# Layer 1's projections cut into half tiles and placed between attention units, with their subtractions on VectorE

## The chip, the cores and the metric

One core of one Trainium2 chip. Times are microseconds (us) of device time for one launch of the whole program. Engines: PE (TensorE matmul; PEld is its weight load), DVE (VectorE), ACT (ScalarE), POOL (GpSimd), SP (SyncE, which issues the loads). A time of day such as 892.30 counts from the first instruction of the profiled execution.

## The reference

A transformer of two layers on 256 latent and 256 context tokens of width 1024, in float32. Layer 0 mixes tokens with a window attention and a latent attention, layer 1 with a differential attention; after each comes a hierarchical mixture of 32 experts (top 2 per token). The change is in the mixer of layer 1:

```
h   = modulate(norm(x))                  512 tokens x 1024
q   = rope(h_lat @ Wq)                   256 latent tokens, 8 heads x (2 x 64)
k   = rope(h @ Wk) for the latent tokens, plain for the context tokens
v   = h @ Wv
for head, for each of 2 blocks of 128 queries:
    a1, a2 = softmax(q1 k1 / 8), softmax(q2 k2 / 8)     128 x 512 each
    o      = (a1 - lambda * a2) @ v                     128 x 128
out = rmsnorm(o) * (1 - lambda_init) @ Wout
```

## The kernel before, in words

**Precision.** Every product with weights is made of three matmuls on two halves of each float32 operand, a rounded one ("hi") and the remainder ("lo"). `mm3` (L395) issues them at L401 to L403, `split` (L385) makes the halves: ACT casts to hi (L391), and DVE or POOL subtracts (L394).

**Buffers and loads.** SBUF holds a pool of 24 buffers of 1 MB. `budget(n)` keeps n of them for data, the rest take weights; SP issues loads in one fixed order whenever a buffer comes free. PSUM has three rotating banks under the name psB, so that the fourth tile put there waits until the first has been read.

**Layer 1's mixer.** The MoE of layer 0 ends, h is made, and then two parts follow each other. First the projections: 12 weight tiles of 1 MB in the order `DWO` (0 to 3 make q, 4 to 7 k, 8 to 11 v). The first is multiplied while h is made (into psA); for each of the others `q_tile`, `k_tile` or `v_tile` (L1687 to L1718) makes two halves, each 24 matmuls of 512 columns (k), 24 of 256 (q) or 48 of 256 (v) into one bank of psB. A finished half of k or q is turned by `rope_lat` (L567): one multiply (L571), four on 32 partitions (L574) and an addition (L575), all on DVE; ACT copies the context half of k (L1683), and `split` with POOL as its engine makes the halves of the result. A finished half of v is copied by ACT (L1716). The next tile's weights are split by `W1.get`, `W1.step` and `W1.make`: two casts of 128x1024 on ACT and two subtractions of 128x1024 on DVE per tile.

Then the attention: `run_units` (L797) goes over 16 units (8 heads, 2 query blocks) as a software pipeline of three stages. One turn does for three neighbouring units: scores (`d_scores`, six matmuls of 512 columns, L1743) and row maxima (DVE, L1750, L1751) of unit i+2; the product with v (`d_pv`, L1787) of unit i-1, with its square on ACT (L1790) and its scaling on DVE (L1791); the combination of the two softmax halves (`d_scale`, DVE, L1765, L1766, L1768) of unit i+1; the transposition (`d_transpose`, L1775, copied by ACT, L1777) of unit i; and the exponentials (ACT, L1758) of unit i+2. `fill()` puts four matmuls of a later table (L323) between them. A hook `early1(i)` sets budgets, splits two tiles of the output projection's weights on POOL (`Wo.step(GP, GP)` at i = 7, 9, 11, 13: L393 and L394 on POOL), and begins the norm of the result (L1799 to L1811) in the last turns.

Then the output projection (`out_block`), the router (`ffn_in`) and the MoE of layer 1, whose expert weights (`in_ew_dram`) stream in until the end.

```
    for j in DWO[1:]:
        (q_tile, k_tile, v_tile)[j // 4](j % 4)
    ...
    run_units([(h, qt) for h in range(8) for qt in range(2)], d_scores, d_max, d_exp, d_scale, d_transpose, d_pv,
              lambda i: i in (1, 2, 3, 14, 15), early1, 3)
```

Of the kernel before, what the change touches and what calls it, by code (L numbers as in the profile page):

```python
# [115 lines left out]
def model_kernel(ctx: ExitStack, tc: tile.TileContext, xin, small, cst, ada0, adaw, win, wuq, wukv, wout0, dwin,  # L116
# [24 lines left out]
    def free(n):  # L141
        st_["data"] -= n
# [41 lines left out]
    def U(shape=(512,), dt=F32):  # L184
        return up.tile([P] + list(shape), dt, tag="u", name="u")
# [7 lines left out]
    def psB():  # L193
        return psb.tile([P, 512], F32, tag="B", name="psB")
# [268 lines left out]
    def xc(c):  # L463
        return xmap[c]
# [99 lines left out]
    DVE.tensor_copy(UB, csv("U"))  # L564


    def rope_lat(ps, dst, p0, cosn, sinn):  # L567

        t = U((SEQ,))
        r = U((SEQ,))  # L570
        DVE.tensor_tensor(t[p0:P], ps[p0:P, 0:SEQ], csv(cosn)[p0:P], ALU.mult)  # L571
        for q in range(p0 // 32, 4):
            a, b = slice(32 * q, 32 * q + 32), slice(32 * (q ^ 1), 32 * (q ^ 1) + 32)
            DVE.tensor_tensor(r[b], ps[a, 0:SEQ], csv(sinn)[a], ALU.mult)  # L574
        DVE.tensor_tensor(dst[p0:P, 0:SEQ], t[p0:P], r[p0:P], ALU.add)  # L575
# [1088 lines left out]
    for c in range(KC):  # L1664
# [13 lines left out]
    DVE.tensor_scalar(nlam, lamt[:, 2:3], -LAMBDA_INIT, None, op0=ALU.add)  # L1678
    k1 = [[S((4, NTOK), F32R) for _ in range(2)] for _ in range(2)]

    def k_out(j, ps):
        dst = U()
        ACT.copy(dst[:, SEQ:], ps[:, SEQ:])  # L1683
        rope_lat(ps, dst, 0, "cosA", "sinA")
        split(*(x[j // 4].v[:, j % 4, :] for x in k1), dst, GP)

    def k_tile(j2):  # L1687
        ws = W1.get()
        for j in range(2):
            ps = psB()  # L1690
            s = slice(j * P, (j + 1) * P)
            mm3(ps, KC, lambda k: (ws[0][:, k, s], ws[1][:, k, s]), h13)
            k_out(2 * j2 + j, ps)
        free(2)

    def q_tile(j2):
        ws = W1.get()
        for j in range(2):
            ps = psB()
            s = slice(j * P, (j + 1) * P)  # L1700
            mm3(ps[:, 0:SEQ], KC, lambda k: (ws[0][:, k, s], ws[1][:, k, s]),
                lambda k: tuple(x[:, 0:SEQ] for x in h13(k)))
            dst = U((SEQ,))
            rope_lat(ps, dst, 0, "cosA", "sinA")
            split(*(x.v[:, 2 * j2 + j, :] for x in q1), dst, GP)
        free(2)

    def v_tile(j):
        ws = W1.get()
        for t2 in range(2):  # L1710
            ps = psB()
            for t in range(2):
                ts_ = slice((2 * t2 + t) * P, (2 * t2 + t + 1) * P)
                mm3(ps[:, t * 256:(t + 1) * 256], KC, lambda k: tuple(x[:, ts_] for x in h13(k)),
                    lambda k: (ws[0][:, k, :], ws[1][:, k, :]))
            ACT.copy(v1[j // 2].v[:, 2 * t2:2 * t2 + 2, (j % 2) * 256:(j % 2 + 1) * 256],  # L1716
                     ps.rearrange("p (t n) -> p t n", t=2))
        free(2)  # L1718
# [8 lines left out]
    free(2)  # L1727
    q1 = [S((KC, SEQ), F32R) for _ in range(2)]
    v1 = [S((4, 512)), S((4, 512))]
    budget(18)  # L1730
    for j in DWO[1:]:
        (q_tile, k_tile, v_tile)[j // 4](j % 4)
    free(4)
    oD = S((16, P))
    budget(11)

    def d_scores(u):
        h, qt = u
# [8 lines left out]
    def d_max(u, ps):  # L1747
        st = T((8,))
        for i in range(2):
            DVE.tensor_reduce(out=st[:, i:i + 1], in_=ps[i], axis=AX.X, op=ALU.max)  # L1750
        DVE.tensor_scalar(st[:, 2:4], st[:, 0:2], -0.125, None, op0=ALU.mult)  # L1751
        return ps, st

    def d_exp(u, ps, st):
        res = []
        for i in range(2):
            pt = U()
            ACT.activation(pt, ps[i], AF.Exp, bias=st[:, 2 + i:3 + i], scale=0.125, accum_out=st[:, 4 + i:5 + i])  # L1758
            res.append(pt)
        return res, st  # L1760
# [21 lines left out]
    def d_pv(u, PTs):  # L1782
        h, qt = u
        PT, rec = PTs
        ps = psB()
        for b in range(4):
            PE.matmul(ps[:, 0:P], PT[:, b * P:(b + 1) * P], v1[h // 4].v[:, b, (h % 4) * P:(h % 4 + 1) * P],  # L1787
                      start=(b == 0), stop=(b == 3))
        sq = U((P,))
        ACT.activation(sq, ps[:, 0:P], AF.Square, scale=rec, accum_out=ssD[:, 0, 2 * h + qt:2 * h + qt + 1])  # L1790
        DVE.tensor_scalar(oD.v[:, 2 * h + qt, :], ps[:, 0:P], rec, None, op0=ALU.mult)  # L1791

# [18 lines left out]
        DVE.scalar_tensor_tensor(out=lo, in0=ps, scalar=sl1, in1=hi.bitcast(F32), op0=ALU.mult, op1=ALU.subtract)  # L1811

    def early1(i):
        if i in {2: 13, 10: 14}:
            budget({2: 13, 10: 14}[i])
        if i == 9:
            free(3)
            budget({2: 13, 10: 14}[10])
        if i in (7, 9, 11, 13):
            Wo.step(GP, GP)  # L1820
        if i == 14:

# [211 lines left out]
```

## Time and profile before

| | us |
|---|---|
| median of three runs | 1468.54 |
| lowest and highest run | 1467.93, 1470.87 |
| the profiled execution's own time | 1465.41 |
| its span, first to last instruction | 1463.6 |
| busy: PE, DVE, ACT, POOL | 1304.4, 582.8, 372.8, 139.6 |
| projections of layer 1, from the second tile's first matmul to the first scores | 789.78 to 892.30 |
| attention, from the first scores to the first matmul of the output projection | 892.30 to 958.33 |

1.8 us of the profiled execution lie around its span, and it is 3.1 us below the median of the runs. The chain of waits names, step by step, what the end of the program hung on; the timeline gives every instruction with its start, its duration and, in brackets, how long its engine had been idle; the table of windows gives each engine's busy time in a stretch, the clock that PE was granted (1.00 is full) and the share of time that the load engines were busy. A matmul's duration in the timeline overlaps the next one's, so PE's pace is read from starts.

### The profile page before, as it was taken

What the parts mean: (1) busy time and instruction counts of PE and PEld (TensorE: products, weight loads), DVE (VectorE), ACT (ScalarE), POOL (GpSimd) and SP (SyncE); (2) the same over time, 40 slices, a digit from 0 to 9 for tenths busy, and PEclk for the clock granted to TensorE, in tenths of its full rate; (3) what the DMA queues carried; (4) which work ended last, traced back from release to release, by engine and by line L of the source; (5) the groups of instructions that cost most, each with busy time, mean ns of one, the idle gap of its engine ahead of it and who ended that gap; (6) DMA issues with size and microseconds to landing.
All of it is one profiled execution on the core that took longest, in us unless ns stands there. A gap on an engine that the chain in (4) does not pass through costs nothing.

```text
span 1463.6 us, 21798 instructions
## 1 busy us (share of the span) xinstructions
PE 1304.4 (89%) x8439; PEld 719.5 (49%) x8439; DVE 582.8 (40%) x1423; ACT 372.8 (25%) x800; POOL 139.6 (10%) x129
## 2 busy tenths in 40 slices
PE   7998999989999989989879999797998786878966
PEld 4775669935435343525226896593442321323313
DVE  6577883454232313222237757945311120111102
ACT  4445653331111110101024334743110100101002
POOL 1122341210000000000013201211000000000000
PEclk9999999999999999999999999999999998998989
DMA  9834443489999999999998138357999999999995
GB/s 381 324 115 145 178 163 151 180 341 371 412 420 420 421 421 421 421 420 421 409 413 342 66 115 320 149 221 296 422 421 421 420 421 421 422 421 422 421 410 225
DMA packets 70253, 486.77 MB, mean 333 GB/s; under 512 B 7681, under 2 KB 7937, under 8 KB 13697
## 3 DMA queue, kind: packets, MB, share of 16 engines
q1 hardware_dynamic: 70144, 485.32, 81.6%
q8 instruction: 69, 1.13, 0.3%
q14 instruction: 40, 0.32, 0.1%
HBM read 484.24 MB, written 1.05 MB: 332 GB/s over the span
## 4 chain that ended last, share of the span: by engine, by line
DMA 26%; PE 15%; DVE 6%; ACT 2%; issue 1%; SPq 0%; DVEq 0%; ACTq 0%
DMA s<-in_ew_dram 25%; PE psA L1358 3%; PE psA L1390 2%; PE psB L402 2%; PE psB L403 2%; PE psB L401 2%; DMA s<-in_adaw_dram 1%; DVE t L1750 1%; DVE u L1768 1%; PE psA L401 1%; PE psA L402 1%; PE psA L403 1%; DVE s L394 1%; DVE u L574 0%; DVE t L1751 0%
## 5 line engine op out<-in xcount | busy, mean ns | idle before, releaser
L1358 PE MATMUL psA<-s 128*32 128x512 f32 (+2 forms) x2336 | 420.0, 624 | 78.1 <-DMA s<-in_ew_dram 72.6
L1358 PEld LDWEIGHTS psA<-s 128*32 128x32 f32 (+2 forms) x2336 | 114.8, 122 | 359.7 <-issue 205.2
L1400 DVE SCALAR_TENSOR_TENSOR s<-psB,modT,s 128x256 f32<-128x256 f32 x296 | 120.4, 476 | 214.3 <-PE psB L1407 214.2
L1390 PE MATMUL psA<-s,u 128*32 128x512 f32 (+1 forms) x1168 | 186.7, 607 | 12.4 <-DMA s<-in_ew_dram 10.9
L1395 DVE SCALAR_TENSOR_TENSOR u<-psA,t,u 128x512 fp32r<-128x512 f32 x48 | 36.0, 750 | 233.1 <-ACT u L1394 233.1
L1390 PEld LDWEIGHTS psA<-s,u 128*32 128x32 f32 (+1 forms) x1168 | 53.7, 120 | 123.6 <-issue 96.7
L1407 PE MATMUL psB<-u 128*128 128x512 f32 (+1 forms) x384 | 95.7, 369 | 13.2 <-DVE s L1400 4.8
L1532 DVE TENSOR_TENSOR u<-u,psA 128x512 f32<-128x512 f32 x24 | 16.5, 687 | 224.1 <-PE psA L1358 224.1
L401 PE MATMUL psB<-s 128*128 128x256 f32 (+1 forms) x304 | 98.8, 325 | 0.2 <-DVE s L890 0.2
L1384 ACT COPY u<-psB 128x512 f32<-128x512 f32 x24 | 14.1, 586 | 332.1 <-PE psB L1382 332.1
L402 PE MATMUL psB<-s 128*128 128x256 f32 (+1 forms) x304 | 98.1, 323 | 0.4 <-DVE s L394 0.4
L403 PE MATMUL psB<-s 128*128 128x256 f32 (+1 forms) x304 | 98.0, 322 | 0.0
L1407 PEld LDWEIGHTS psB<-u 128*128 128x128 f32 x384 | 58.8, 188 | 72.4 <-issue 36.0
L1394 ACT ACTIVATE u<-psA,t 128x512 fp32r<-128x512 f32 x48 | 33.0, 687 | 177.4 <-PE psA L1390 171.8
L1529 ACT ACTIVATE u<-psA 128x512 f32<-128x512 f32 x24 | 14.4, 598 | 219.4 <-PE psA L1358 219.4
L1341 PE MATMUL psB<-s 128*128 128x256 f32 x544 | 68.0, 285 | 0.6 <-ACT u L1384 0.6
L394 DVE TENSOR_TENSOR s<-s 128x1024 fp32r<-128x1024 f32 (+3 forms) x56 | 51.6, 966 | 39.2 <-ACT s L391 39.1
L1341 PEld LDWEIGHTS psB<-s 128*128 128x128 f32 x544 | 65.9, 191 | 2.6 <-issue 1.6
L401 PEld LDWEIGHTS psB<-s 128*128 128x128 f32 x304 | 57.9, 190 | 8.3 <-issue 1.7
L402 PEld LDWEIGHTS psB<-s 128*128 128x128 f32 x304 | 57.9, 190 | 4.8 <-DVE s L394 0.7
L403 PEld LDWEIGHTS psB<-s 128*128 128x128 f32 x304 | 57.9, 190 | 4.5
L401 PE MATMUL psA<-s 128*128 128x256 f32 (+1 forms) x200 | 58.7, 294 | 0.0
(354 smaller groups left out, 1706.5 us busy)
## 6 DMA issues: line engine op xcount, KB each, us to landing
s<-in_ew_dram SPq DMA_DIRECT2D x376, 1024.0 KB, 19.8
s<-in_adaw_dram SPq DMA_DIRECT2D x40, 1024.0 KB, 6.6
s<-in_dwin_dram SPq DMA_DIRECT2D x12, 1024.0 KB, 10.5
s<-in_ada_dram SPq DMA_DIRECT2D x8, 1024.0 KB, 17.5
s<-in_wout_dram SPq DMA_DIRECT2D x8, 1024.0 KB, 8.6
s<-in_ew_dram SPq DMA_DIRECT2D x16, 512.0 KB, 14.6
s<-in_win_dram SPq DMA_DIRECT2D x4, 1024.0 KB, 20.9
s<-in_xin_dram SPq DMA_DIRECT2D x4, 512.0 KB, 5.0
```

Of the source, the lines that this page charges most:

```text
L394: eng.tensor_tensor(lo, src, hi.bitcast(F32), ALU.subtract)
L401: PE.matmul(ps, lh, rh, start=(k == 0), stop=False)
L402: PE.matmul(ps, lh, rl, start=False, stop=False)
L403: PE.matmul(ps, ll, rh, start=False, stop=(k == n - 1))
L1341: PE.matmul(ps[:, i * n:(i + 1) * n], src(t, cs_(c0 + i)), oh[:, t, 0:n], start=(t == 0 and a == 0), stop=(t == T_ - 1 and a == 1))
L1358: PE.matmul(ps[sl, :], xg(hf * 4 + k, sl), wt(m, hf)[:, k, :], start=(hf == 0 and k == 0), stop=(hf == 1 and k == 3))
L1390: PE.matmul(ps[sl, :], ht[:, k, sl], wt(2, hf)[:, k, :], start=(k == 0), stop=(k == 3))
L1394: ACT.activation(yh, ps, AF.Copy, scale=gsl)
L1395: DVE.scalar_tensor_tensor(out=yl, in0=ps, scalar=gsl, in1=yh.bitcast(F32), op0=ALU.mult, op1=ALU.subtract)
L1400: DVE.scalar_tensor_tensor(out=xc(c)[:, HALF[s]], in0=ps[:, HALF[s]], scalar=modT[:, l, 5, c, s:s + 1], in1=xc(c)[:, HALF[s]], op0=ALU.mul ...
L1407: PE.matmul(ps[:, 0:nt], ysp[a][:, cs_(q)], oht[:, 0:nt], start=(a == 0), stop=(a == 1))
L1532: TT(hm, sl, pm[1], ALU.mult)
```

## The change

- The projections of tiles 2 to 12 become 22 half tiles, called pieces. A piece is the matmuls of one half into one bank of psB, followed by `W1.step()`, which splits half of the weights of the tile after it (cast on ACT, subtraction on DVE). Its rope or copy (`evacs`) is issued at the start of the next turn, the halves of its result (`splits`) at that turn's end.
- Of tiles 2 to 12 only six halves still precede the unit loop: two halves of q come first, then the scores of units 0 and 1 between two halves of k, two more halves of q, and the other 16 halves stand in turns 0 to 12 of the unit loop, by the table `PIECES`. `DWO` is reordered so that each head's q, k and v come shortly before their use.
- The subtractions that make the lo halves of q and k move from POOL to DVE (8 of 128x512, 8 of 128x256).
- `rope_lat`'s temporaries, q's result and the squares of `d_pv` go to a free half of an old tensor (`room()`), not to the pool of small tiles.
- `Wo.step(GP, GP)` moves from turns 7, 9, 11, 13 to the ends of turns 12 to 15; the fills from three before the loop and turns 1, 2, 3, 14, 15 to turns 2, 6, 11, 13, 14, 15; the budgets to 19 before the attention, 16 at turn 9 and 14 at turn 14 (before 18, 11, 13, 14).

The diff, cut to its core:

```diff
+PIECES = {0: 2, 1: 1, 2: 1, 3: 1, 4: 2, 5: 2, 6: 1, 7: 1, 8: 2, 9: 1, 10: 1, 12: 1}
-DWO = (4, 5, 6, 8, 0, 7, 9, 1, 10, 2, 11, 3)
+DWO = (4, 0, 5, 1, 8, 9, 6, 2, 10, 7, 3, 11)
...
-        split(*(x[j // 4].v[:, j % 4, :] for x in k1), dst, GP)
+        split(*(x[j // 4].v[:, j % 4, :] for x in k1), dst)
...
+    def k_piece(j2, j, ws):
+        ps = psB()
+        s = slice(j * P, (j + 1) * P)
+        mm3(ps, KC, lambda k: (ws[0][:, k, s], ws[1][:, k, s]), h13)
+        dst = []
+
+        def evac():
+            dst.append(U())
+            k_rope(dst[0], ps)
+        return evac, lambda: k_split(2 * j2 + j, dst[0])
...
+    def piece(n=1):
+        for _ in range(n):
+            j, i = pieces.pop(0)
+            if i == 0:
+                cur.append(W1.get(False))
+            made.append((q_piece, k_piece, v_piece)[j // 4](j % 4, i, cur[0]))
+            W1.step()
+            if i:
+                cur.pop()
+                free(2)
...
-    budget(18)
-    for j in DWO[1:]:
-        (q_tile, k_tile, v_tile)[j // 4](j % 4)
-    free(4)
     oD = S((16, P))
-    budget(11)
...
+    piece(2)
+    evacs()
+    splits()
+    for i in range(2):
+        piece()
+        mx1[i] = d_max(units[i], d_scores(units[i]))
+        ex1[i] = d_exp(units[i], *mx1.pop(i))
+    evacs()
+    pts1[0] = d_scale(units[0], ex1.pop(0))
+    splits()
+    piece(2)
+    for i in range(n_u + 1):
+        evacs()
+        if i + 2 < n_u:
+            mx1[i + 2] = d_max(units[i + 2], d_scores(units[i + 2]))
+        early1(i)
+        if 0 < i:
+            d_pv(units[i - 1], PT1.pop(i - 1))
+        if i in (2, 6, 11, 13, 14, 15):
+            fill()
+        if i + 1 < n_u:
+            pts1[i + 1] = d_scale(units[i + 1], ex1.pop(i + 1))
+        if i < n_u:
+            PT1[i] = d_transpose(units[i], pts1.pop(i))
+        if i + 2 < n_u:
+            ex1[i + 2] = d_exp(units[i + 2], *mx1.pop(i + 2))
+        splits()
+        if i in (12, 13, 14, 15):
+            Wo.step(GP, GP)
+        piece(PIECES.get(i, 0))
```

Lines of the changed kernel are two (in the helpers) to some 30 higher than before: the subtraction of `split` is L396 (before L394), the rope L572, L575, L576 (before L571, L574, L575), the scores L1775, the maxima L1782 and L1783, `d_scale` L1797 to L1800, the transposition L1807, `d_pv`'s scaling L1823.

DVE's order from the weights of the second tile on, before (128x8x128 is half a weight tile, that is 128x1024; the first two ropes read psA and belong to the first tile):

```order
L394 TENSOR_TENSOR s<-s 128x8x128 x2
L571 TENSOR_TENSOR u<-psA,u 128x256
L574 TENSOR_TENSOR u<-psA,u 32x256 x4
L575 TENSOR_TENSOR u<-u 128x256
L571 TENSOR_TENSOR u<-psA,u 128x256
L574 TENSOR_TENSOR u<-psA,u 32x256 x4
L575 TENSOR_TENSOR u<-u 128x256
L394 TENSOR_TENSOR s<-s 128x8x128 x2
L571 TENSOR_TENSOR u<-psB,u 128x256
```

and in the changed kernel:

```order
L396 TENSOR_TENSOR s<-s 128x8x128 x2
L572 TENSOR_TENSOR s<-psA,u 128x256
L575 TENSOR_TENSOR s<-psA,u 32x256 x4
L576 TENSOR_TENSOR u<-s 128x256
L396 TENSOR_TENSOR s<-u,s 128x512
L572 TENSOR_TENSOR s<-psA,u 128x256
L575 TENSOR_TENSOR s<-psA,u 32x256 x4
L576 TENSOR_TENSOR u<-s 128x256
L396 TENSOR_TENSOR s<-u,s 128x512
L396 TENSOR_TENSOR s<-s 128x8x128 x2
L572 TENSOR_TENSOR s<-psB,u 128x256
```

The two new rows are k's subtractions (128x512), each after its rope; the third tile's weights come behind both.

DVE a little later in the changed kernel, where the maxima of units 0 and 1, the rest of the third and the fourth tile's weights, and the ropes of two halves of k follow each other (s<-s 128x256 x2 are q's subtractions); before, no unit's work stands among the ropes:

```order
L396 TENSOR_TENSOR s<-s 128x256 x2
L396 TENSOR_TENSOR s<-s 128x8x128
L1782 TENSOR_REDUCE t<-psA 128x1 x2
L1783 TENSOR_SCALAR t<-t 128x2
L396 TENSOR_TENSOR s<-s 128x8x128
L1782 TENSOR_REDUCE t<-psA 128x1 x2
L1783 TENSOR_SCALAR t<-t 128x2
L572 TENSOR_TENSOR s<-psB,u 128x256
L575 TENSOR_TENSOR s<-psB,u 32x256 x4
L576 TENSOR_TENSOR u<-s 128x256
```

The rope of the first of these halves of k now stands behind two units' maxima and two weight subtractions.

PE's order in the middle of the attention before, two whole turns:

```order
L1775 MATMUL psB<-identR,u 128x128 x4
L1743 MATMUL psA<-s 128x512 x6
L1787 MATMUL psB<-s,u 128x128 x4
L1775 MATMUL psB<-identR,u 128x128 x4
L1743 MATMUL psA<-s 128x512 x6
L1787 MATMUL psB<-s,u 128x128 x4
```

and in the changed kernel where the second half of tile 1 (q) ends, turn 0 runs, and the first half of tile 8 (v) begins:

```order
L405 MATMUL psB<-s 128x256
L1775 MATMUL psA<-s 128x512 x6
L1807 MATMUL psB<-identR,u 128x128 x4
L403 MATMUL psB<-s 128x256
L404 MATMUL psB<-s 128x256
L405 MATMUL psB<-s 128x256
```

Scores of unit 2 and the transposition of unit 0 stand between 24 matmuls of a half of q and 48 of a half of v.

## Rows read from the trace of the kernel before

**Rows 1.** windows: length, busy PE, PEld, DVE, ACT, POOL, then PEclk, DMA, GB/s

```profile
850.00:875.00 25.00, 25.00 (x211) 25.00 (x210) 13.78 (x22) 8.26 (x11) 1.48 (x2) 1.00 0.29 88
900.00:925.00 25.00, 19.66 (x130) 12.54 (x130) 23.88 (x41) 13.01 (x37) 14.43 (x8) 0.89 0.80 322
925.00:950.00 25.00, 22.69 (x155) 15.78 (x153) 22.31 (x59) 21.93 (x64) 0.00 (x0) 0.98 0.31 117
1100.00:1436.00 336.00, 268.13 (x1446) 90.67 (x1444) 48.65 (x122) 28.17 (x50) 1.90 (x1) 0.93 1.01 420
```

**Rows 2.** timeline of PE (start, duration): k and q halves, scores, last product with v

```profile
789.78 0.39 PE L401 MATMUL psB<-s 128*128 128x512 f32 x1
795.22 0.39 PE L401 MATMUL psB<-s 128*128 128x512 f32 x1
...
877.33 0.28 PE L403 MATMUL psB<-s 128*128 128x256 f32 x1
880.21 0.28 PE L403 MATMUL psB<-s 128*128 128x256 f32 x1
...
892.30 1.65 PE L1743 MATMUL psA<-s 64*128 64x512 f32 x12
893.88 2.78 PE L323 MATMUL psC<-s,scS 128*32 128x512 f32 x24
...
954.98 1.06 PE L1787 MATMUL psB<-s,u 128*128 128x128 f32 x8
```

**Rows 3.** timeline of PE in one turn of the attention

```profile
907.01 0.66 PE L1775 MATMUL psB<-identR,u 128*128 128x128 f32 x4
907.60 0.96 PE L1743 MATMUL psA<-s 64*128 64x512 f32 x6
908.49 1.16 PE L1787 MATMUL psB<-s,u 128*128 128x128 f32 x8
909.58 1.06 PE L323 MATMUL psC<-s,scS 128*32 128x512 f32 x8
```

**Rows 4.** chain of waits in order of time, one turn apart

```profile
930.64 0.75 DVE u L1768
933.41 0.75 DVE u L1768
```

**Rows 5.** timeline of DVE, ACT and POOL where the projections begin

```profile
788.69 2.36 DVE L394 TENSOR_TENSOR s<-s 128x1024 fp32r<-128x1024 f32 x2
790.97 0.42 DVE L571 TENSOR_TENSOR u<-psA,u 128x256 f32<-128x256 f32 x1
793.16 0.42 DVE L575 TENSOR_TENSOR u<-u 128x256 f32<-128x256 f32 x1
793.66 0.62 ACT L391 CAST s<-u 128x512 fp32r<-128x512 f32 x1 [3.81 <-issue]
797.99 1.30 POOL L394 TENSOR_TENSOR s<-u,s 128x512 fp32r<-128x512 f32 x1 [2.34 <-ACT s L391]
798.90 1.47 DVE L394 TENSOR_TENSOR s<-s 128x1024 fp32r<-128x1024 f32 x1 [1.70 <-ACT s L391]
```

**Rows 6.** groups by line and form, 790 to 990: count, busy, mean ns

```profile
L394 POOL TENSOR_TENSOR s<-u,s 128x512 fp32r<-128x512 f32 x8 | 10.4, 1294 | 33.1 <-ACT s L391 33.1
L575 DVE TENSOR_TENSOR u<-u 128x256 f32<-128x256 f32 x16 | 6.8, 425 | 0.6
L1803 DVE TENSOR_TENSOR s<-s,ssD 128x512 f32<-128x512 f32 x4 | 2.7, 685 | 0.0
```

**Rows 7.** timeline while POOL splits the output projection's weights

```profile
910.82 2.37 POOL L394 TENSOR_TENSOR s<-s 128x1024 fp32r<-128x1024 f32 x1 [2.56 <-PE psC L323]
911.02 2.71 DVE L1768 SCALAR_TENSOR_TENSOR u<-u,t 128x512 f32<-128x512 f32 x1
921.19 1.12 PE L1775 MATMUL psB<-identR,u 128*128 128x128 f32 x4 [4.77 <-DVE u L1768]
```

**Rows 8.** windows, just after PE's idle 4.77

```profile
920.00:926.00 6.00, 4.78 (x19) 3.42 (x20) 5.89 (x9) 2.00 (x6) 4.39 (x3) 0.50 0.10 18
```

More of the change, by code (lines that the diff above doesn't have):

```diff
@@ L50 @@
 ADL = 3
-DWO = (4, 5, 6, 8, 0, 7, 9, 1, 10, 2, 11, 3)
-ADO = {0: (0, 1), 1: (2, 3, 4), 2: (5,), 3: (6,), 4: (7,)}
+PIECES = {0: 2, 1: 1, 2: 1, 3: 1, 4: 2, 5: 2, 6: 1, 7: 1, 8: 2, 9: 1, 10: 1, 12: 1}
+DWO = (4, 0, 5, 1, 8, 9, 6, 2, 10, 7, 3, 11)
+ADO = {0: (0, 1), 1: (2, 3, 4), 6: (5,), 9: (6,), 11: (7,)}
 NFIX = (4, 4)
@@ L564, in model_kernel, with rope_lat @@
     DVE.tensor_copy(UB, csv("U"))
-    def rope_lat(ps, dst, p0, cosn, sinn):
-        t = U((SEQ,))
-        r = U((SEQ,))
+    def rope_lat(ps, dst, p0, cosn, sinn, tr=None):
+        t, r = tr or (U((SEQ,)), U((SEQ,)))
         DVE.tensor_tensor(t[p0:P], ps[p0:P, 0:SEQ], csv(cosn)[p0:P], ALU.mult)
@@ L1672, in model_kernel @@
     h_lo(1, KC - 1, xb, *h13(KC - 1), True)
+    budget(19)
     fill(2)
@@ L1679, in model_kernel, with room, k_rope @@
     k1 = [[S((4, NTOK), F32R) for _ in range(2)] for _ in range(2)]
+    rooms_ = [0]
+    def room():
+        rooms_[0] += 1
+        return xc(rooms_[0] % KC)[:, SEQ:]
+    def k_rope(dst, ps):
+        ACT.copy(dst[:, SEQ:], ps[:, SEQ:])
+        rope_lat(ps, dst, 0, "cosA", "sinA", (room(), room()))
     def k_out(j, ps):
         dst = U()
-        ACT.copy(dst[:, SEQ:], ps[:, SEQ:])
-        rope_lat(ps, dst, 0, "cosA", "sinA")
-        split(*(x[j // 4].v[:, j % 4, :] for x in k1), dst, GP)
@@ L1687, in k_tile @@
[L1687 to L1718, printed above, removed]
+        k_rope(dst, ps)
@@ new lines, in k_out, with k_split, q_piece @@
+        k_split(j, dst)
+    def k_split(j, dst):
+        split(*(x[j // 4].v[:, j % 4, :] for x in k1), dst)
[8 more added lines that the diff above has]
+        return evac, lambda: k_split(2 * j2 + j, dst[0])
+    def q_piece(j2, j, ws):
+        ps = psB()
+        s = slice(j * P, (j + 1) * P)
+        mm3(ps[:, 0:SEQ], KC, lambda k: (ws[0][:, k, s], ws[1][:, k, s]),
+            lambda k: tuple(x[:, 0:SEQ] for x in h13(k)))
+        dst = room()
+        tr = (room(), room())
+        return (lambda: rope_lat(ps, dst, 0, "cosA", "sinA", tr),
+                lambda: split(*(x.v[:, 2 * j2 + j, :] for x in q1), dst))
@@ new lines, in v_piece @@
+    def v_piece(j, t2, ws):
+        ps = psB()
+        for t in range(2):
+            ts_ = slice((2 * t2 + t) * P, (2 * t2 + t + 1) * P)
+            mm3(ps[:, t * 256:(t + 1) * 256], KC, lambda k: tuple(x[:, ts_] for x in h13(k)),
+                lambda k: (ws[0][:, k, :], ws[1][:, k, :]))
+        return (lambda: ACT.copy(v1[j // 2].v[:, 2 * t2:2 * t2 + 2, (j % 2) * 256:(j % 2 + 1) * 256],
+                                 ps.rearrange("p (t n) -> p t n", t=2)), lambda: None)
+    pieces = [(j, n) for j in DWO[1:] for n in range(2)]
@@ L1720, in model_kernel, with evacs, splits @@
+    cur, made = [], []
+    def piece(n=1):
[8 more added lines that the diff above has]
+                free(2)
+    def evacs():
+        for e, _ in made:
+            e()
+    def splits():
+        for n in range(len(made)):
+            made.pop(0)[1]()
     wl = [W1.get(False)]
@@ L1788, in d_pv @@
                       start=(b == 0), stop=(b == 3))
-        sq = U((P,))
+        sq = room()[:, 0:P]
         ACT.activation(sq, ps[:, 0:P], AF.Square, scale=rec, accum_out=ssD[:, 0, 2 * h + qt:2 * h + qt + 1])
@@ L1813, in early1 @@
     def early1(i):
-        if i in {2: 13, 10: 14}:
-            budget({2: 13, 10: 14}[i])
         if i == 9:
             free(3)
-            budget({2: 13, 10: 14}[10])
-        if i in (7, 9, 11, 13):
-            Wo.step(GP, GP)
+            budget(16)
+        if i == 14:
+            free(4)
+            budget(14)
         if i == 14:
@@ L1831, in early1 @@
             d_turn(1)
-    run_units([(h, qt) for h in range(8) for qt in range(2)], d_scores, d_max, d_exp, d_scale, d_transpose, d_pv,
-              lambda i: i in (1, 2, 3, 14, 15), early1, 3)
+    units = [(h, qt) for h in range(8) for qt in range(2)]
+    n_u, ex1, mx1, pts1, PT1 = len(units), {}, {}, {}, {}
+    piece(2)
[28 more added lines that the diff above has]
+        piece(PIECES.get(i, 0))
     d_rstd(12, 16)
```

## The prediction

> **What bounds the kernel now.** I read the table of windows first. From 1100 to 1436 the load engines are busy all the time (1.01, 420 GB/s) and PE is not [rows 1]: layer 1's MoE waits for its expert weights, so nothing saved there counts. It can start only when the mixer before it is done, and the pool of buffers is full by then; so a microsecond that the mixer gains or loses moves the end by about one. The mixer has two regimes. In the projections PE is the bound: 25.00 of 25 busy, DVE 13.78 [rows 1]. In the attention DVE is: 22.31 and 23.88 of 25, PE 22.69 and 19.66 [rows 1]. The change mixes the two.
>
> Next PE's timeline, for its pace (from starts, since durations overlap). A half of k takes 795.22 - 789.78 = 5.44 us, a half of q 880.21 - 877.33 = 2.88, and a half of v, twice q's matmuls, 5.76; a unit's scores half of 893.88 - 892.30, 0.79 [rows 2]. A transposition is 0.59, a product with v 1.09, a fill about 1.0 [rows 3]. So a unit is 2.47 us of PE. The chain shows the pitch of an undisturbed turn, 933.41 - 930.64 = 2.77, carried by DVE [rows 4].
>
> Then DVE's timeline where the projections begin: half a tile's weight subtraction 1.18 (2.36 for two), a rope 2.61 (790.97 to 793.58), of which 2.18 until it has read its bank [rows 5].
>
> **The change, part by part.** PE's own work from 789.78 to the last product with v: six halves of k 32.6, eight of q 23.0, eight of v 46.1, 16 units 39.5, six fills 6.0; together 147.2. Nothing of this is removed: only waits can go. Without any, the last product would end at 937.0; before, it ends at 956.0 [rows 2].
>
> To see the waits I laid the new order end to end by hand: three queues (PE, DVE, ACT), each block in its place in the changed order, starting when its engine is free and 0.12 after its inputs (ACT's cast starts 0.08 after the rope that it reads [rows 5]). DVE's blocks besides those above: a unit's two maxima with their scaling 1.40 and its combination 1.11, which with 0.26 for the product's scaling make the 2.77.
>
> The new subtractions on DVE are not in the trace. The nearest rows are additions on DVE, 0.685 for 128x512 and 0.425 for 128x256 [rows 6]: eight of each are at most 8.9 us, and at least nothing, where DVE would be idle anyway. I lay them at 0.64 and 0.40, a little under, because consecutive instructions of DVE overlap by some 0.03: 8.3 us.
>
> The start. At 788.69 DVE has before it: the second tile's weights 2.36; two halves of k of the first tile, each now rope 2.61, a wait for ACT's cast 0.8, subtraction 0.64, 4.0 in all; then the third tile's first half of weights 1.18. That is 800.3 (788.69 + 2.36 + 8.1 + 1.18). PE, which has two halves of q meanwhile, is done with them at 795.5 and wants those weights: a wait of 5.0. Before, PE had a whole tile of k (10.9) at this place to cover it.
>
> Next come the other half of these weights, two ropes of q, q's subtractions, the fourth tile's weights, two maxima and the rope of the first half of k: scores 0 wait 1.4, and the second half of the next tile of q, which takes the bank of that half of k, three places behind it, waits 3.2. Then two ropes, a combination, subtractions, weights: the first half of v waits for the bank of q's half until 830.7, 5.2; the transposition before it 0.5. Altogether PE has done 25.4 us of work by then, and waited 15.3. DVE's queue, not PE's, sets this stretch: 37 us of blocks in 42.
>
> The middle: in turns 3 to 9 the same happens on a smaller scale wherever halves of k and q follow each other: 0.6, 1.3, 3.6 (the weights of a tile of v stand behind two ropes), 0.6, 1.3, 2.1 (scores 12 wait for the subtraction of q made a turn before), 1.2: 10.7. From turn 13 on no projections are left, and each turn waits 1.0, as before, DVE being the bound: 3.1. Smaller ones 1.0. Waits in all 30.1, so the last product ends at 967.3.
>
> The same lay-out of the kernel before ends at 946.7, where the trace has 956.0. Up to unit 3 it is within 1 us; what it lacks is the 7 us that POOL costs, and 2.3 of the norm in the last turns. Like for like the change costs 967.3 - 946.7 = **20.6**.
>
> POOL's seven: while it subtracts 128x1024 (2.37), DVE's combination takes 2.71 instead of 0.75, and PE then stands idle 4.77 [rows 4, 7]. The changed order sends these four steps later: two fall beside halves of v, on which PE has work for 5.76, two into the last turns. Below, 0 (all hidden); above, 7 as before; I take 3, since half of them meet turns without cover. So 7 are returned and 3 paid.
>
> SP's loads: as many as before, the mixer's twelve in another order; those behind them are released later, because the projections hold their buffers longer. The expert weights that fill the pool are at most some 23 MB, about 55 us at 420 GB/s [rows 1]; the attention's last turns, the output projection and the router, in which they can come, are about as long. I price this at 0, up to 3 if the pool is not full.
>
> The ropes' temporaries in the free half of an old tensor: same instructions, 0. The fills are moved, not removed: 0.
>
> Sum: 20.6 - 7 + 3 = 16.6. Against the profiled execution's 1465.41 this is 1482.0. That execution lies 3.1 below the median, so the median I forecast is **1485**.
>
> **A rule against the change.** POOL's subtraction beside DVE's makes DVE's 1.47 instead of 1.18 [rows 5], and POOL is nearly idle in the projections, 1.48 of 25 [rows 1]. With q's and k's subtractions left on POOL (1.29 [rows 6], and for half the width some 0.7) my lay-out ends at 966.4, 0.9 earlier. The Trainium skill, Perfetto Trace Analysis, section "Optimizing Scalar/DVE Operations", says that if VectorE is saturated it may pay to give work away, even to GPSIMD, but warns that those two share a read port. By its first half the sum would be 15.7 and not 16.6, by its second the 0.29 is the price of that; either way the choice of engine decides less than the order.
>
> **The rivals.**
>
> *Interleaving works* (faster). DVE is busy 13.8 of 25 in one regime and about 23.1 in the other [rows 1]: of 102.5 us of projections and 66 of attention 56 and 61, with the new subtractions 126 us of DVE against 147.2 of PE. If DVE's backlog never reaches PE, the 30.1 of waits go, apart from the last turns' 3.1: 1485 - 27 = 1458. The sign turns where waits fall under 13.5 (30.1 - 16.6). For it: the totals; the weights are split a tile ahead. Against: up to the first half of v DVE has one and a half times PE's work, and three banks let PE run ahead by three halves only. The Trainium skill, Perfetto Trace Analysis, "Optimization Strategy", says that kernels with several regimes may gain by interleaving them; by that rule this case would be the outcome.
>
> *Half of it* (no change). The lay-out overstates the waits by two, at the start and in the middle alike, because a bank or a weight half comes free earlier than I count: 15 are left, about 1470.
>
> *The clock falls* (slower still). After 4.77 idle PE was granted 0.50, the level of 1.2 GHz, for 6 us [rows 7, 8], and a transposition took 1.12 instead of 0.66 [rows 3, 7]. Two waits here are as long. If each is followed by 6 us at half pace, 3 us each, and POOL costs its whole 7, it is 1485 + 6 + 4 = 1495.
>
> *Not what it says*: the weights are a whole tile ahead only in the middle; at the start the third tile's wait for DVE is part of the forecast. I give it no chance of its own.
>
> **How the numbers follow.** Forecast 0.58, its own range 1477 to 1493 (hand-over 0.05 or 0.2: -2.5, +3; POOL 0 to 7; loads 0 to 3). The clock 0.12, interleaving works 0.18, half of it 0.12. The range that leaves out 2 in 10 is 1464 to 1495: it loses most of the interleaving case above and a little of the clock's. A measurement can tell 0.2% here, 2.9 us; 1465.6 to 1471.5 is "same". Half of the "half of it" case lies there; its rest is split between the sides. Faster 0.21, same 0.06, slower 0.73.
>
> **What would show it.** Right: in PE's timeline, idle of about 5 us before the first half of k of the third tile, released by the weight subtraction on DVE, and of 3 to 5 us before the second tile of q and the first half of v, released by ropes; DVE busy 90% from 790 to 830; output projection at about 970 to 973; MoE loads back to back until about 1453. Wrong: PE's busy share over 95% from 790 to 950, with the output projection before 955; or the first projections waiting for something other than DVE, a load of weights above all; or the end moving by another amount than the start of the output projection.

## The result, and the profile after

| | before | after |
|---|---|---|
| median of five runs, us | 1468.54 | 1481.76 |
| lowest, highest | 1463.05, 1470.87 | 1478.95, 1484.62 |
| the profiled execution's own time | 1465.41 | 1481.76 |

The ratio is 1.008, with an interval of 1.0059 to 1.0102: **slower by 9 to 15 us**. The forecast was 1485, in a range of 1464 to 1495.

The page's first lines after:

```profile
span 1480.0 us, 21765 instructions
PE 1309.3 (88%) x8439; PEld 723.4 (49%) x8439; DVE 589.1 (40%) x1439; ACT 372.6 (25%) x800; POOL 122.9 (8%) x113
```

One window over the whole stage, from the first matmul of the second tile to the first of the output projection, shows the difference best. Before (length, then busy PE, PEld, DVE, ACT, POOL, granted clock, load share, GB/s):

```profile
789.78:958.33 168.55, 155.93 (x1089) 131.58 (x1088) 124.20 (x244) 76.80 (x172) 30.68 (x24) 0.98 0.46 174
```

and after, where the stage begins 3.4 later (MoE 0 before it ends at a slightly different time in each execution, 786.4 to 793.3 in the profiles of this study, so stages are compared by their own length):

```profile
793.22:974.86 181.64, 161.01 (x1089) 134.21 (x1088) 131.47 (x258) 76.70 (x172) 13.99 (x8) 0.96 0.37 134
```

The stage grew from 168.55 to 181.64, by 13.1. PE's idle time in it grew from 12.6 to 20.6, by 8.0, and its busy time by 5.1, with the same 1089 matmul instructions (seven fills in each): its granted clock is 0.96 instead of 0.98. From the output projection's first matmul to the last instruction it is 505.3 before and 505.1 after: what the stage loses, the end loses, as the chain shows, which still ends with expert weights back to back:

```profile
1412.84 20.43 DMA s<-in_ew_dram
1433.29 19.87 DMA s<-in_ew_dram
1453.20 3.63 PE psA L1391 x26
```

PE's idle time in its timeline of the changed kernel (start, duration, instruction, and in brackets the idle time before it and who ended it); these answer to [rows 2, 3]:

```profile
802.92 0.79 PE L403 MATMUL psB<-s 128*128 128x512 f32 x1 [3.74 <-ACT s L393]
824.74 0.36 PE L403 MATMUL psB<-s 128*128 128x256 f32 x1 [2.54 <-DVE s L575]
831.46 0.38 PE L403 MATMUL psB<-s 128*128 128x256 f32 x1 [0.67 <-ACT u L1809]
832.42 0.39 PE L404 MATMUL psB<-s 128*128 128x256 f32 x1 [0.58 <-DVE s L396]
...
890.05 0.39 PE L403 MATMUL psB<-s 128*128 128x256 f32 x1 [3.01 <-ACT s L393]
891.31 0.58 PE L404 MATMUL psB<-s 128*128 128x256 f32 x1 [0.87 <-DVE s L396]
...
934.67 1.25 PE L1775 MATMUL psA<-s 64*128 64x512 f32 x6 [1.15 <-ACT s L393]
...
966.88 0.63 PE L1840 MATMUL psB<-identR,s 128*128 128x128 f32 x4 [1.94 <-DVE s L1835]
```

Each is a place of the lay-out: the third tile's first half of k behind its weights (forecast 5.0, measured 3.7), the second half of q behind a rope (3.2, 2.5), the first half of v (5.2, and here 0.7 + 0.6), a half of v behind its weights (3.6, 3.0 + 0.9), scores 12 behind the halves of q (2.1, 1.2, released by ACT's cast). What the lay-out did not have is the clock. In the windows after three of these waits (columns as above) it is at 0.50, the level of 1.2 GHz, or on its way:

```profile
802.00:805.00 3.00, 2.04 (x4) 1.23 (x5) 2.75 (x3) 1.82 (x2) 0.00 (x0) 0.52 0.44 186
805.00:808.00 3.00, 3.00 (x8) 2.32 (x8) 2.85 (x8) 0.05 (x1) 0.00 (x0) 0.50 0.00 0
...
826.00:829.00 3.00, 3.00 (x16) 2.88 (x14) 2.80 (x8) 1.13 (x2) 0.00 (x0) 0.50 0.01 3
...
890.00:893.00 3.00, 2.07 (x9) 1.87 (x10) 2.95 (x4) 0.95 (x2) 0.00 (x0) 0.64 0.79 236
```

With the rows beside these (0.84 from 808 to 811, 0.79 from 893 to 896) busy time at the lower level cost about 6 us, an estimate from these windows (3.0 of 805 to 808 at half pace are 1.5, and so on). A part of the first half of v's forecast wait went there: PE was slower and came later. The half also came free sooner than the lay-out had it, 38.2 after the stage's first matmul (831.46 - 793.22) and not 40.9 (830.7 - 789.78).

Why PE waits at 802.92 is seen in the timeline of ACT and DVE ahead of it; the rows of before are [rows 5]:

```profile
797.17 0.62 ACT L393 CAST s<-u 128x512 fp32r<-128x512 f32 x1 [3.87 <-issue]
797.82 0.69 DVE L396 TENSOR_TENSOR s<-u,s 128x512 fp32r<-128x512 f32 x1 [0.73 <-ACT s L393]
800.79 0.43 DVE L576 TENSOR_TENSOR u<-s 128x256 f32<-128x256 f32 x1
801.30 0.62 ACT L393 CAST s<-u 128x512 fp32r<-128x512 f32 x1 [3.25 <-DVE u L576]
801.83 1.99 ACT L393 CAST s<-s 128x1024 fp32r<-128x1024 f32 x2
801.95 0.69 DVE L396 TENSOR_TENSOR s<-u,s 128x512 fp32r<-128x512 f32 x1 [0.74 <-ACT s L393]
802.90 1.23 DVE L396 TENSOR_TENSOR s<-s 128x1024 fp32r<-128x1024 f32 x1 [0.25 <-ACT s L393]
```

Both queues hold the third tile's weights behind the second rope of k: ACT casts them at 801.83, after the cast of that rope's result, and DVE subtracts them at 802.90, after its subtraction. What releases PE at 802.92 is the first of ACT's casts, not DVE's subtraction. The new subtractions took 0.69 and 0.42 each (0.64 and 0.40 were assumed).

POOL's four subtractions are still there. One lay beside turn 11 of the changed kernel:

```profile
947.28 2.38 POOL L396 TENSOR_TENSOR s<-s 128x1024 fp32r<-128x1024 f32 x1 [9.29 <-PE psC L325]
947.35 2.85 DVE L1800 SCALAR_TENSOR_TENSOR u<-u,t 128x512 f32<-128x512 f32 x1
950.25 0.66 PE L1807 MATMUL psB<-identR,u 128*128 128x128 f32 x4 [0.57 <-DVE u L1800]
...
951.43 2.17 DVE L1783 TENSOR_SCALAR t<-t 128x2 f32<-128x2 f32 x1
```

DVE's combination took 2.85 instead of 0.75, as it took 2.71 before [rows 7], but PE, with scores and a product to do, waited only 0.57 and not 4.77; the 2.17 of a turn later, under POOL's second subtraction, lies behind a half of v. The fourth, in the last turns, stretched a combination too:

```profile
961.23 2.93 DVE L1800 SCALAR_TENSOR_TENSOR u<-u,t 128x512 f32<-128x512 f32 x1
964.31 0.63 PE L1807 MATMUL psB<-identR,u 128*128 128x128 f32 x4 [0.78 <-DVE u L1800]
```

### The profile page after: what moved, and what is told of

The parts are those of the page before. It is cut to its first block, busy times and chain, and to the rows that moved or that the text cites. A ratio compares the mean times of both kernels' runs of the same rounds, so it can differ in the third digit from the quotient of the medians.

```text
span 1480.0 us, 21765 instructions
## 1 busy us (share of the span) xinstructions
PE 1309.3 (88%) x8439; PEld 723.4 (49%) x8439; DVE 589.1 (40%) x1439; ACT 372.6 (25%) x800; POOL 122.9 (8%) x113
## 4 chain that ended last, share of the span: by engine, by line
DMA 25%; PE 17%; DVE 6%; ACT 2%; issue 1%; DVEq 0%; SPq 0%; ACTq 0%
DMA s<-in_ew_dram 25%; PE psA L1359 3%; PE psA L1391 2%; PE psB L403 2%; PE psB L404 2%; PE psB L405 2%; DVE s L575 1%; DVE s L396 1%; PE psB L1819 1%; PE psA L1775 1%; ACT s L393 1%; PE psA L403 1%; PE psA L404 1%; PE psA L405 1%; ACT u L1790 0%
## 5 line engine op out<-in xcount | busy, mean ns | idle before, releaser
L403 PE MATMUL psB<-s 128*128 128x256 f32 (+1 forms) x304 | 102.7, 338 | 13.2 <-ACT s L393 6.7
L1408 PE MATMUL psB<-u 128*128 128x512 f32 (+1 forms) x384 | 95.7, 369 | 13.2 <-DVE s L1401 4.6
L404 PE MATMUL psB<-s 128*128 128x256 f32 (+1 forms) x304 | 100.5, 331 | 1.5 <-DVE s L396 1.5
L405 PE MATMUL psB<-s 128*128 128x256 f32 (+1 forms) x304 | 100.5, 331 | 0.0
L403 PEld LDWEIGHTS psB<-s 128*128 128x128 f32 x304 | 59.6, 196 | 24.0 <-ACT s L393 7.2
L1342 PEld LDWEIGHTS psB<-s 128*128 128x128 f32 x544 | 65.9, 192 | 2.6 <-issue 1.6
L396 DVE TENSOR_TENSOR s<-s 128x1024 fp32r<-128x1024 f32 (+3 forms) x64 | 54.3, 884 | 29.6 <-ACT s L393 29.4
L404 PEld LDWEIGHTS psB<-s 128*128 128x128 f32 x304 | 59.8, 197 | 6.1 <-DVE s L396 1.9
L405 PEld LDWEIGHTS psB<-s 128*128 128x128 f32 x304 | 59.7, 196 | 5.5 <-DVE s L396 0.8
```

Source lines behind the costliest of these rows:

```text
L1342: PE.matmul(ps[:, i * n:(i + 1) * n], src(t, cs_(c0 + i)), oh[:, t, 0:n], start=(t == 0 and a == 0), stop=(t == T_ - 1 and a == 1))
L1408: PE.matmul(ps[:, 0:nt], ysp[a][:, cs_(q)], oht[:, 0:nt], start=(a == 0), stop=(a == 1))
```

## The experiments

Theory A: DVE and ACT work their queues in order, and the changed order puts the next tile's weights, a half at a time, behind ropes that themselves wait for PE; PE waits for them. B: it is the 16 subtractions on VectorE. C: POOL and DVE slow each other. D: it is the clock after the waits. E: it is the interleaving as such. All times are medians; "stage" is the stretch above, in the run's one profiled execution. e1 to e4, e5 to e8 and e9 to e11 were each measured beside the kernel before (medians 1469.8, 1469.4 and 1468.4), so runs of different groups are best compared by their ratios.

| run | median | ratio to before, interval | stage |
|---|---|---|---|
| before | 1468.5 | | 168.6 |
| changed | 1481.8 | 1.008, 1.0059 to 1.0102 | 181.6 |
| e1_subs_pool | 1486.2 | 1.0116, 1.0099 to 1.0132 | 189.6 |
| e2_pair_split | 1475.1 | 1.0038, 1.0018 to 1.0058 | 177.0 |
| e3_v_first | 1484.7 | 1.0105, 1.0088 to 1.0122 | 187.3 |
| e4_warm | 1481.0 | 1.0079, 1.0059 to 1.0100 | 181.1 |
| e5_upfront | 1489.8 | 1.0150, 1.0133 to 1.0167 | 191.7 |
| e6_upfront_pair | 1479.8 | 1.0078, 1.0061 to 1.0095 | 181.8 |
| e7_before_subs_dve | 1470.8 | 1.0017, 1.0006 to 1.0029 | 173.4 |
| e8_before_wo_dve | 1464.6 | 0.9972, 0.9957 to 0.9987 | 167.6 |
| e9_before_wo_min | 1462.9 | 0.9958, 0.9941 to 0.9974 | 165.8 |
| e10_pair_wo_dve (e2's kernel again) | 1469.8, one run | | 176.3 |
| e11_pair_wo_dve | 1479.2 | 1.0075, 1.0054 to 1.0095 | 180.1 |

### Whose subtractions: e1 and e7

```diff
-        split(*(x[j // 4].v[:, j % 4, :] for x in k1), dst)
+        split(*(x[j // 4].v[:, j % 4, :] for x in k1), dst, GP)
...
-                lambda: split(*(x.v[:, 2 * j2 + j, :] for x in q1), dst))
+                lambda: split(*(x.v[:, 2 * j2 + j, :] for x in q1), dst, GP))
```

> The changed kernel with the subtractions of q's and k's results on POOL again, nothing else. Theory A (DVE's in-order queue holds PE up, through the order of its blocks): the 8.3 us that leave DVE are mostly not the ones waited for; the same lay-out gives 0.9 less, so about 1481, between 1479 and 1483. Rival B (it is the 16 subtractions on VectorE): the loss goes, about 1470 to 1474. Rival C (POOL beside DVE slows the weight subtractions, 1.47 instead of 1.18): nothing or slower, 1482 to 1485.

It was slower than the change, 1486.2 (the intervals of the two ratios just touch; the stage is 189.6 against 181.6): B falls, C holds, and A's range of 1479 to 1483 was missed. In the timeline of e1 POOL's subtraction of 128x256 beside DVE's of 128x1024 took 1.78, and scores 12 waited for it; behind that wait PE was granted 0.50 to 0.61 from 934 to 946, where the change has 1.00 (timeline, and one window):

```profile
933.87 1.23 DVE L396 TENSOR_TENSOR s<-s 128x1024 fp32r<-128x1024 f32 x1 [1.90 <-ACT s L393]
933.89 1.78 POOL L396 TENSOR_TENSOR s<-s 128x256 fp32r<-128x256 f32 x1
935.73 0.80 PE L1775 MATMUL psA<-s 64*128 64x512 f32 x2 [2.05 <-POOL s L396]
```

```profile
938.00:942.00 4.00, 3.33 (x16) 2.92 (x16) 2.67 (x7) 2.69 (x8) 0.28 (x1) 0.50 0.06 20
```

By an estimate from the windows of these 12 us the lower clock cost about 4, so the wait and the clock behind it make most of the 8 us by which the stage is longer. DVE's weight subtractions took 1.30 on average there against 1.22 in the change. The other way round, the same subtractions moved to DVE in the kernel before (the two lines above with their `GP` taken out):

> The kernel before with the 16 subtractions of q's and k's results on DVE. Theory A: 8.7 us more on DVE (0.69 and 0.42 each in the changed kernel's trace), in projections where DVE is busy 13.8 of 25: 0 to +3, 1468 to 1472. Rival B (the subtractions on VectorE are what costs): +8 to +13, 1477 or more.

1470.8, 1 to 4 us over before: as A has it. In the projections DVE has room for them: 102.8 us against 102.5. What its profiled execution has more lies at the start of the attention, where scores 2 waited 2.30 instead of 0.81 and the clock was 0.73 and 0.70 in the 12 us after; why, no run shows.

### Where the weights are split: e2, e5 and e6

```diff
-            W1.step()
+            if i == 0:
+                W1.step()
+                W1.step()
```

> The changed kernel with both halves of the next tile's weights split at a tile's first piece instead of one at each piece. Theory A: weight subtractions come ahead of ropes in DVE's queue; the lay-out ends 4.8 earlier, mostly in the middle, where a half of v waited for its weights (3.0 at 890): 1477, between 1474 and 1479. Rival (interleaving costs what it costs, wherever the weights are split): 1482.

1475.1: 6.7 less than the change, and the stage 4.7 less, where A said 4.8. The waits of PE by releaser (total, times, longest) in the change and in e2:

```profile
PE psB L403 <- ACT s L393: 6.7, 2, 3.7
```

```profile
PE psB L403 <- ACT s L393: 3.7, 1, 3.7
```

The one at 890 is gone, with its slow clock; the one at 802 is left. e10 is the same kernel once more, beside e11: its single run 1469.8, 3 under its forecast of 1473 to 1477, its stage 176.3 against 177.0.

To take the interleaving away and leave the split in halves, e5 puts all 22 pieces ahead of the attention, in the order of tiles of before (the edit's core; the budget at turn 9 is 14 again, as before, and the buffers freed at turn 14 are freed ahead of the loop; the places of the fills and of `Wo.step` stay those of the change):

```diff
-PIECES = {0: 2, 1: 1, 2: 1, 3: 1, 4: 2, 5: 2, 6: 1, 7: 1, 8: 2, 9: 1, 10: 1, 12: 1}
+PIECES = {}
-DWO = (4, 0, 5, 1, 8, 9, 6, 2, 10, 7, 3, 11)
+DWO = (4, 5, 6, 8, 0, 7, 9, 1, 10, 2, 11, 3)
...
+    for _ in range(22):
+        piece()
+        evacs()
+        splits()
+    free(4)
+    budget(11)
+    for i in range(2):
+        mx1[i] = d_max(units[i], d_scores(units[i]))
+        ex1[i] = d_exp(units[i], *mx1.pop(i))
+    pts1[0] = d_scale(units[0], ex1.pop(0))
```

> The pieces of the changed kernel, all 22 ahead of the attention, in the order of tiles of before, each with its rope and subtraction right behind it; so no interleaving, but half a tile of the next weights split at each piece, on DVE behind the piece's predecessor's rope, and the subtractions on DVE. Budgets as before. Theory A (order in DVE's queue): the second half of a tile's weights stands behind a rope that itself waits for PE; the same lay-out has PE wait 5.7 before the first v and 3.0 before each other v, plus 6 at the first scores, which no fill covers: 964.9 against 948.1 for the kernel before; 1479 to 1486. Rival E (interleaving as such costs the time): as before, 1467 to 1471.

> The same with both halves of the next tile's weights split at a tile's first piece. Theory A: the waits before v go, the 6 at the first scores stays: 951.2 in the lay-out, 3 more than before; 1468 to 1473. Rival E: as e5, 1467 to 1471 in both.

e5 is the slowest of all, 1489.8, without any interleaving (4 over A's range, with an attention of 73.0 instead of 66.0, for the reasons given for e6 below); e6, the same with `W1.step()` twice at a tile's first piece, 1479.8. E falls as the cause of e5, and the split in halves alone is worth 10 us in the medians, 15.7 in the projections themselves (118.7 against 103.1). In e5 PE waits before each tile of v for its weights (4.6 once and 1.2 three times, each with 0.7 or 0.9 behind it), of which the first:

```profile
815.90 0.58 PE L403 MATMUL psB<-s 128*128 128x256 f32 x1 [4.55 <-ACT s L393]
817.16 0.58 PE L404 MATMUL psB<-s 128*128 128x256 f32 x1 [0.68 <-DVE s L396]
```

In e6 none of these is left but one of 0.9, and the projections take 103.1 us (892.73 - 789.68) as before (102.5). But e6 was forecast at 1468 to 1473, and that missed by 7. Its attention takes 78.7 instead of 66.0:

```profile
899.39 2.31 PE L1777 MATMUL psA<-s 64*128 64x512 f32 x6 [5.01 <-ACT u L1792]
928.42 1.12 PE L1809 MATMUL psB<-identR,u 128*128 128x128 f32 x4 [3.98 <-DVE u L1802]
948.46 1.12 PE L1809 MATMUL psB<-identR,u 128*128 128x128 f32 x4 [3.96 <-DVE u L1802]
```

The first is the wait that the three fills ahead of the loop covered before (forecast 6); the other two are units behind POOL's subtractions, at 922.0 to 927.8 and 942.1 to 947.9, and after each of the three the clock was 0.50 for 6 us. So most of the 12.7 is put down to the new places of the fills and of `Wo.step`, where no projections stand between units; this is read from the waits, and no run moves these places alone. `Wo.step` moved in the program to turns 12 to 15, but POOL has nothing else queued, and its first subtraction ran at 922.0, beside unit 6's transposition, six turns ahead of its place. What it waits for is a fill: it starts as the fill of turn 6 ends, and the third as that of turn 11 does:

```profile
940.86 1.06 PE L325 MATMUL psC<-s,scS 128*32 128x512 f32 x8
942.10 2.36 POOL L396 TENSOR_TENSOR s<-s 128x1024 fp32r<-128x1024 f32 x1 [7.50 <-PE psC L325]
```

A fill gives its weights' buffer back. It was so before, where the fill of turn 3 released the first of the four [rows 3, 7], and in the change, at 947.28 above, behind the fill of turn 11. So it is the fills' places that set when POOL begins to disturb DVE.

These runs also bear on the rival that interleaving helps. e5 and the change, and e6 and e2, differ in it, in the order of tiles and in the budgets, and the interleaved one is the faster both times: 1.0150 against 1.008, 1.0078 against 1.0038, some 10 and 6 us. So the interleaving covers waits that other parts of the change bring, and the loss against the kernel before lies in those parts.

### The start: e3 and e4

```diff
-PIECES = {0: 2, 1: 1,
+PIECES = {1: 1,
-DWO = (4, 0, 5, 1, 8, 9, 6, 2, 10, 7, 3, 11)
+DWO = (4, 8, 0, 5, 1, 9, 6, 2, 10, 7, 3, 11)
...
     piece(2)
     evacs()
     splits()
+    piece(2)
+    evacs()
+    splits()
```

> The changed kernel with the first tile of v moved ahead of the first tile of q, so that PE has 11.5 us of matmuls while DVE works off k's ropes and the weights; turn 0 loses its two pieces for it. Theory A: the wait of 3.7 at 802 goes with its slow clock, another comes at units 0 and 1 (4 to 5 in two places); in sum the lay-out ends 6.6 earlier: 1475, between 1473 and 1478. Rival (the start is not what costs): 1482.

This missed: 1484.7, no faster than the change (the stage is 187.3 against 181.6). The wait at 802 is gone, as A says, but unit 1's transposition, now without pieces around it, waits for all of DVE's backlog at once, and then PE runs at half pace (timeline, and a window after it):

```profile
842.85 1.12 PE L1807 MATMUL psB<-identR,u 128*128 128x128 f32 x4 [7.57 <-DVE u L1800]
```

```profile
844.00:848.00 4.00, 4.00 (x20) 4.00 (x20) 2.92 (x8) 2.95 (x8) 0.00 (x0) 0.50 0.00 0
```

The forecast had 4 to 5 in each of two places there and no clock. So moving the wait does not remove it: the backlog of DVE has to be worked off, and this transposition is the next thing in PE's queue. (Of its profiled execution's 1490.3, some 6 lie after the stage, at a lower clock in the last turns of the MoE; its median has less of that.)

```diff
+    def warm(n):
+        a = h13(0)[0]
+        ps = [psA(), psA()] if n else []
+        for m in range(n):
+            PE.matmul(ps[m % 2], a[:, 0:P], a, start=True, stop=True)
...
             j, i = pieces.pop(0)
+            warm({(5, 0): 15, (10, 0): 12}.get((j, i), 0))
```

> The changed kernel with 15 matmuls of 512 columns, whose results nothing reads, ahead of the first half of k of tile 5 and 12 ahead of the first half of v of tile 10, where PE waited 3.7 and 3.0: 3.4 and 2.7 us of PE in time that was idle. Rival D (the granted clock, 0.50 from 802 to 809 and 0.64 after 890, is what the waits cost): 3 to 5 us come back, 1477 to 1479. Theory A: the scores after that half of k wait for the subtraction of q on DVE at 811.5 whatever PE's clock; PE runs faster and waits the more: 1481 to 1482, clock in this stretch 1.00.

1481.0, as the change: A's time came out, and D's 3 to 5 us did not. The clock stayed at 1.00 from 800 to 810, and the scores then waited for DVE's subtraction of q:

```profile
800.00:810.00 10.00, 8.37 (x36) 5.71 (x34) 8.74 (x17) 3.25 (x6) 0.00 (x0) 1.00 0.23 94
```

```profile
810.03 0.50 PE L1782 MATMUL psA<-s 64*128 64x512 f32 x2 [0.82 <-DVE s L396]
822.97 0.36 PE L403 MATMUL psB<-s 128*128 128x256 f32 x1 [2.81 <-DVE s L575]
```

PE reached the next wait, for the rope, earlier and waited 2.8 instead of 2.5. Counted from the stage's first matmul, the first half of v starts at 37.4 instead of 38.2: of the 3 us that the slow clock cost from 802 to 811, 0.8 came back. Behind 890 it is another matter: scores 12 come at 139.3 (931.63 - 792.29) instead of 141.5 (934.67 - 793.22), 2.1 earlier and so 1.3 more, about all that this slow stretch had cost. That the stage as a whole is 181.1 and not 179.5 lies in its last turns, where this execution fell to a lower clock after a wait of 1.94 that in the change had 1.00 behind it:

```profile
931.63 1.25 PE L1782 MATMUL psA<-s 64*128 64x512 f32 x6 [1.15 <-ACT s L393]
963.85 0.88 PE L1847 MATMUL psB<-identR,s 128*128 128x128 f32 x4 [1.94 <-DVE s L1842]
```

```profile
963.00:967.00 4.00, 3.15 (x16) 2.52 (x20) 2.09 (x5) 1.15 (x3) 0.00 (x0) 0.64 1.02 424
```

So the slow clock at 802 is mostly covered by DVE's backlog, and the one at 890 is a cost of its own. The medians are too coarse for the 2 us in question, and the slow stretch after the rope at 824 was not warmed.

### POOL's share: e8, e9 and e11

```diff
-            Wo.step(GP, GP)
+            Wo.step(DVE, GP)
```

> The kernel before with POOL's four subtractions of the output projection's weights on DVE (1.2 each; the casts stay on POOL). If POOL's subtractions cost the 7 us that were read from the trace of before, DVE's turns grow by 4.8 instead of 7 and no turn waits 4.8 at a time, so the clock stays at 1.00: 1464 to 1467. Rival (they are hidden or cost nothing): DVE's 4.8 come on top, 1472 to 1475.

1464.6, in the kernel before: 2 to 6 us faster, where the forecast's 7 us for POOL less 4.8 for DVE gives 2.2. The waits of units for DVE's combination, before and in e8:

```profile
PE psB L1775 <- DVE u L1768: 8.7, 9, 4.8
```

```profile
PE psB L1775 <- DVE u L1768: 7.5, 11, 1.7
```

No turn waits 4.8 any more, and from 921 to 927 the clock is 1.00 where it was 0.57. It did not stay up everywhere: from 946 to 957.5 it is 0.85. Going on from there:

```diff
-        if i in (7, 9, 11, 13):
-            Wo.step(GP, GP)
+        if i in (7, 9):
+            Wo.step(DVE, GP)
...
-            ws = Wo.get(False)
+            ws = Wo.get(c == 0)
```

> The kernel before with one tile of the output projection's weights made in the attention (casts on POOL, subtractions on DVE, turns 7 and 9) and the second one made by ACT and DVE while the first is multiplied, where DVE is busy 10 of 27 us. If DVE's turns are what the attention takes, two subtractions of 1.2 leave it: 2 to 3 under e8_before_wo_dve, 1461 to 1463. Rival (the output projection waits for the second tile): as e8 or slower, 1464 to 1468.

1462.9, faster than both kernels, by 4 to 9 us against before; the second tile's weights are made under the output projection. Against e8 the step is 1.7, less than the two runs can tell apart.

> A second look at the changed kernel with both halves split at a tile's first piece, beside e11 on the same chip: 1473 to 1477.

> The changed kernel with both halves split at a tile's first piece, and POOL's four subtractions of the output projection's weights on DVE. Two of the four fall beside halves of v, where PE covers them, two in the last turns, where DVE's combination took 2.85 instead of 0.75: 2 to 4 under e2_pair_split, 1471 to 1473, still above the kernel before, since the start's waits (3.7, 2.5, 1.2) and its slow clock stay. Rival (POOL is hidden in the changed order): 1475 as e2.

e11 (e2 with the same line as e8) missed: 1479.2, not 1472. In the changed order the four steps stand at the ends of the last turns, and DVE's own subtraction there came ahead of the norm on which the next transposition depends:

```profile
957.95 1.22 DVE L396 TENSOR_TENSOR s<-s 128x1024 fp32r<-128x1024 f32 x1
959.09 1.29 DVE L1837 TENSOR_TENSOR s<-s,ssD 128x512 f32<-128x512 f32 x2
959.92 1.09 PE L1842 MATMUL psB<-identR,s 128*128 128x128 f32 x4 [3.90 <-DVE s L1837]
```

PE waited 3.9 where it had waited 1.9, and was granted 0.50 from 960 to 965. It is the mechanism of the start again: what counts is what stands ahead in DVE's queue. What POOL's subtractions cost in the changed order e11 can't tell, since it brings this wait with it.

## Why the prediction was right

- **That PE's waits for DVE decide, and where.** Right in the main: of the nine waits over 1 us that were forecast ahead of turn 13, eight are in the trace at their places, seven of them shorter; only that of the half of v at 890 is not (3.9, forecast 3.6). The ninth, the scores' 1.4, is not there, but 0.8 in e4, where the clock was not low ahead of it. e2, e5 and e6 show the mechanism: where a half of the next weights stands in the queues decides 7 to 10 us. Three of the signs did not come as stated: PE was released at 802.92 by ACT's cast of the weights, not by DVE's subtraction; the first half of v waited 0.7 + 0.6 and not 3 to 5; and DVE was busy 77% from 790 to 830, not 90%.
- **The size, partly by luck.** Like for like 16.6 was forecast, 13.1 was the stage's growth and 13.2 the medians'. The forecast had 30.1 us of waits, the trace has 20.6 of idle, and beside them some 6 of slow clock, which the prediction left out of its sum and gave to a rival. The two errors point in opposite ways. They are two forms of one backlog only in part: in e4 the clock's 3 us at the start were mostly covered by later waits, its 1.3 behind 890 were not.
- **POOL: 7 returned and 3 paid.** The 3 were too many. PE waited 0.57 at turn 11, and in the last turns 0.73, 0.78 and 1.94 (the last for the norm, which the lay-out leaves out), 3.5 in all where the lay-out has 3.1 without POOL: so about 1 was paid. What POOL had cost before was not measured by itself; some 4 us (e8) and 5.5 (e9) come back when DVE does its subtractions, which fits a 7 of which DVE takes a part.
- **The new subtractions.** 8.7 us on DVE instead of 8.3, and in the kernel before they cost 1 to 4 us (e7), not 13: the choice of engine is not the cause. The lay-out said 0.9 in POOL's favour; e1 says 4.5 against it. Here the step failed that left POOL's subtractions undisturbed: beside DVE's they took up to 1.79 instead of 0.74, and stood on the path of scores 12. The Trainium skill, Perfetto Trace Analysis, "Optimizing Scalar/DVE Operations", warns that giving DVE's work to GPSIMD may not help, as the two share a read port; e1 agrees, with 1486.2 against 1481.8.
- **Loads.** Priced at 0, and 505.1 against 505.3 us from the output projection to the end bears it out.
- **Rivals.** That interleaving lets PE run through did not happen: PE is idle 20.6 us of the stage. The Trainium skill, Perfetto Trace Analysis, "Optimization Strategy", says that interleaving regimes may help; the runs agree where little else differs (the change against e5, e2 against e6), but against the kernel before they show no gain: e2, the best interleaved version, is still 1.0038 of it. PE's idle time in the stage before is 12.6 us of 168.55, of which e9, by POOL's steps alone, leaves 9.4 (165.79 less 156.36 busy). There was little for interleaving to fill.
- **Left open.** What of the remaining 6 us of e2 over before is the start, what the last turns and what the slow clock was not separated by a run, nor were the fills' new places tried alone; and a start with DVE's work halved was not tried.

## What to carry to other kernels

Before cutting work into finer pieces, lay each engine's queue end to end: an instruction that prepares the next tile must not stand behind one that waits for the present tile. Totals of busy time do not show this; one half-tile of look-ahead instead of a whole one cost 10 us in a stage of some 180 without any interleaving. And look for the engine that slows another one before rearranging: moving POOL's four subtractions to DVE, in the order before, brought 4 us, and none of the interleaved orders tried here was faster than the one before.

## What was not expected of the hardware

- POOL and DVE stretch each other in both directions: a subtraction of 128x256 on POOL took 0.74 alone and 1.78 beside DVE's of 128x1024 (e1), and a scaling of only 128x2 on DVE 0.17 alone and 2.17 beside POOL's of 128x1024.
- 15 matmuls whose result nobody reads kept the granted clock at 1.00 through a wait of 3.7 us and brought back 0.8 of the 3 us that the slow clock had cost there, since the next waits for DVE took up the rest; 12 more, ahead of a half of v behind which PE had work, brought back about all of 1.4. So the clock was worth buying where PE was what the next step waited for.
